# A hybrid encoder layer on one core: the merge of three branches in a written order, with eight gate tiles ahead of it

## The chip, the core and the metric

The kernel runs on one core of a Trainium2 chip. The core has five engines that work side by side: TensorE (PE, matrix products into the PSUM banks), VectorE (DVE), ScalarE (ACT), GpSimd (POOL) and SyncE (SP), which here issues all DMAs, in order, to sixteen DMA engines. Each engine works through its own queue in order and waits on semaphores for the others. The metric is the time of one execution in microseconds (us) of the device; the kernel before takes 2960.99 us, the median of three runs (2956.82 to 2964.68).

## The reference

One layer of a bidirectional encoder over 1280 tokens (a sequence of 1024 and one of 256), D_MODEL = 1024, in float32. Three mixers read the same normalised input, each is gated, and their sum goes through an output projection and a gated feed-forward network:

```python
h = rms_norm(x, p['norm_mix_g'][l])
proj = h @ p['w_in'][l]                       # split among the mixers and the gates
o_a = blocked_attention(q, k, v_a, MLA_QK ** -0.5).reshape(B, T, H * MLA_V) @ p['w_o_a'][l]
# RWKV-7, both directions, then a norm per head:
y7 = y_f + y_b
mu = jnp.mean(y7, axis=-1, keepdims=True)
var = jnp.mean(jnp.square(y7 - mu), axis=-1, keepdims=True)
y7 = ((y7 - mu) * lax.rsqrt(var + LNX_EPS)).reshape(B, T, RW_DIM)
y7 = y7 * p['lnx_g'][l].astype(F32) + p['lnx_b'][l].astype(F32)
o_b = (y7 * g7).astype(x.dtype) @ p['w_o_b'][l]
o_c = jnp.einsum('bhqk,bkhd->bqhd', pr.astype(mv.dtype), mv).reshape(B, T, X_DIM) @ p['w_o_c'][l]
gates = jax.nn.sigmoid(gate_logits.astype(F32)).reshape(B, T, N_BRANCH, D_MODEL).astype(x.dtype)
merged = gates[:, :, 0] * o_a + gates[:, :, 1] * o_b + gates[:, :, 2] * o_c
x = x + merged @ p['w_out'][l]
up = rms_norm(x, p['norm_ffn_g'][l]) @ p['w_up'][l]
# ... centred convolution of width 3 on the gate half, gelu, product, w_down
```

## The kernel before

Activations lie with the features on the 128 partitions and the tokens along the free axis; the tokens are cut into three chunks, CH: chunk 0 and chunk 1 of 512 tokens and chunk 2 of 256. Each product of float32 values is done as three matmuls of a split into a high and a low part (`mm3`, lines 133 to 135); `split` makes the parts, the cast on ACT (line 126), the difference on POOL or DVE (line 129). `load_w` (line 139) loads a weight tile by DMA and splits it.

The work comes in stages: the input projections (to about 670 us), then RWKV's scan with attention and gate tiles put between its steps (to 1648 us), the merges of the three branches (to 1936 us), the output projection (to about 2053 us) and the feed-forward network. Between stages the intermediates go through DRAM: `oaT`, `ocT` and `yS` are the mixers' outputs (attention A, cross-attention C, RWKV B), `rden` the reciprocals of the softmax sums, `gT` the gate logits, `obT` the normalised RWKV output.

RWKV's PE instructions stand in an order that the program works out beforehand: the class `Order` keeps a model time, takes the ready lane of RWKV, and where none is ready it takes the next step of a filling generator, first attention and the gate tiles of chunk 1 (`fill`), then the spare gate tiles of chunk 0 (`spare`, lines 900 to 911). A gate tile is one of 24 groups of 128 output features; in one of 512 tokens there are 24 matmuls, yielded in steps of three k, each counted as 512 x 3.6 / 1024 = 1.8 us by the planner. Before, sixteen tiles of chunk 0 (16 to 23, then 8 to 15) are on the list `g0`, and `spare` stops when four of them are left. Everywhere outside RWKV the order of the instructions on each engine is made by the compiler's list scheduler from a simulated timeline.

The merges (`merges`, line 1739; called from `phase2`): for each branch and each output tile m = 0 to 7, and for each chunk, `merge` forms `w_o` times the branch's input in PSUM (`mg_ps`), and DVE multiplies it by the gate (line 1728), which is loaded from `gT` into `mg` (line 1721) and put through tanh. The inputs are loaded by `merge_in`: a chunk of `oaT` or `ocT` (line 1699, tile `mf`, two buffers), the reciprocals, broadcast to two halves of 64 partitions (line 1704, tile `mrd`), their product on DVE (line 1707), and the split into `moh` and `mol`. Branch A comes first; between its products stand the last gate tiles: four before m = 0, one for each m whose result stays in SBUF (`keep=True`), so its chunk 0 is merged with no trip through DRAM.

`rwkv_out` (from line 1642) finishes one of the ten RWKV tiles of 128 tokens: loads of the two directions (lines 1648 and 1650, `oy` with two buffers) and of v (line 1653), the norm on DVE, POOL and ACT (lines 1661 to 1672), four PE transposes (`yt`, line 1676), scaling on ACT (1682), the product with g7 on POOL (1685) and a store into `obT`. One is called for each m of branch A and for the first two of C. Branch B, which needs all ten, is merged last; its input loads begin inside branch C.

Of the kernel before, what the change touches and what calls it, by code (L numbers as in the profile page):

```python
# [97 lines left out]
class Kern:  # L98
# [813 lines left out]

    def gates(self, p, pp):

        self.wp = p
        self.g0 = [*range(16, 24), *range(8, 16)]
        self.h[0] = self.h[1] = tuple(p.tile([128, 8, 512], F32R, name=f"gh{x}") for x in "hl")
        w = self.load_w(p, self.io["w_g"][0], [128, 8, 128], "w4", sbufs=2)
        self.gates_h(p, 1)
        yield -10.0  # L920
        for m in range(24):
            for x in self.gate_(p, pp, "at", m, 1, "go", 3, w=w):
                yield x if isinstance(x, float) else 512 * 2.4 / 1024
            w = None
# [718 lines left out]
    def rwkv_out(self, p, pr, i):  # L1643
# [14 lines left out]
        def bc(t):  # L1658
            return t.unsqueeze(2).to_broadcast([128, 8, 64])
# [29 lines left out]
    def merge_in(self, p, br, src, fs, bufs):  # L1689

        nc, io = self.nc, self.io
        for f in fs:
            oh = p.tile([128, T], F32R, tag="moh", name="moh", bufs=bufs)
            ol = p.tile([128, T], F32R, tag="mol", name="mol", bufs=bufs)
            for ci in (1, 2, 0):
                c0, cn = CH[ci]
                cs = slice(c0, c0 + cn)
                t = p.tile([128, 512], F32, tag="mf", name="mf", bufs=2)
                nc.sync.dma_start(out=t[:, :cn], in_=src[f][:, cs])
                if br != 1:  # L1700
                    rd = p.tile([128, 512], F32, tag="mrd", name="mrd", bufs=2)
                    for e in range(2):
                        r = 2 * f + e if br == 0 else 8 + f
                        nc.sync.dma_start(
                            out=rd[64 * e : 64 * e + 64, :cn], in_=io["rden"][r : r + 1, cs].to_broadcast([64, cn])
                        )
                    nc.vector.tensor_mul(out=t[:, :cn], in0=t[:, :cn], in1=rd[:, :cn])
                self.split(t[:, :cn], oh[:, cs], ol[:, cs], "act", "dve" if ci == 1 else "pool")
            yield oh, ol

    def merge_w(self, p, br, m):
        return self.load_w(p, self.io["w_o"][br][m], [128, 4, 128], "wo", sbufs=1)

    def merge(self, p, br, m, ci, w, o, merged, parts, pp, g=None):

        nc, io = self.nc, self.io
        c0, cn = CH[ci]
        cs = slice(c0, c0 + cn)
        if g is None:
            g = p.tile([128, 512], F32, tag="mg", name="mg", bufs=5 if br == 1 else 3)  # L1720
            nc.sync.dma_start(out=g[:, :cn], in_=io["gT"][br * 8 + m][:, cs])
            nc.scalar.activation(out=g[:, :cn], in_=g[:, :cn], func=AF.Tanh, scale=0.5)
        ps = pp.tile([128, 512], F32, tag="mp", name="mg_ps")
        for k in range(4):
            self.mm3(ps[:, :cn], w[0][:, k, :], w[1][:, k, :], o[k][0][:, cs], o[k][1][:, cs], k == 0, k == 3)
# [10 lines left out]
                out=lo, in0=t, scalar=0.5, in1=hi.bitcast(F32), op0=ALU.mult, op1=ALU.subtract  # L1736
            )

    def merges(self, gp, ro, mg, pp, merged):


        io = self.io

        def gate(m, keep=False):
            return self.gate(gp, pp, "mp", m, 0, "go", 3, keep)

        def gate0():
            if self.g0:
                gate(self.g0.pop(0))

        o = list(self.merge_in(mg, 0, io["oaT"], range(4), 6))
        for m in range(8):
            if m == 0:
                for _ in range(4):
                    gate0()
            w = self.merge_w(mg, 0, m)
            for ci in (1, 2):
                self.merge(mg, 0, m, ci, w, o, merged, None, pp)
            self.rwkv_out(ro, pp, m)
            g = gate(m, True)  # L1760
            self.merge(mg, 0, m, 0, w, o, merged, None, pp, g)
            gate0()
            if m == 3:
                oc = list(self.merge_in(mg, 2, io["ocT"], range(2), 6))
        for m in range(4):
            gate0()
        oc += self.merge_in(mg, 2, io["ocT"], range(2, 4), 6)
        for m in range(8):
            if m < 2:
                self.rwkv_out(ro, pp, 8 + m)  # L1770
            if m == 4:
                yield
            w = self.merge_w(mg, 2, m)
            for ci in (1, 2):
                self.merge(mg, 2, m, ci, w, oc, merged, None, pp)
            if m < 4:
                gate0()
            self.merge(mg, 2, m, 0, w, oc, merged, None, pp)


    def out_proj(self, p, x1, h2, pp):
# [157 lines left out]
    def phase2(self, rctx):  # L1939
# [8 lines left out]
        def close():  # L1948
            pools.pop().__exit__(None, None, None)
# [5 lines left out]
        with self.pool("pat", space=PSUM, bufs=3) as pa:  # L1955
# [14 lines left out]
            gctx, gp = ctx  # L1970
            close()
            x1 = left("x1").tile([128, 8, T], F32, name="x1")
            ro, mg = left("ro"), left("mgac")
            with self.pool("pmg", space=PSUM, bufs=5) as pm:
                rest = self.merges(gp, ro, mg, pm, x1)
                next(rest)
                gctx.__exit__(None, None, None)
                rctx.__exit__(None, None, None)
                wctx, mw = right("mgw")
                bctx, mb = right("mgb")  # L1980
                w = self.merge_w(mw, 1, 0)
                o = list(self.merge_in(mb, 1, io["obT"], range(4), 4))
                for _ in rest:
                    pass
                close()
                close()
                hp = left("h2")
# [4 lines left out]
                self.wu = left("wu")  # L1992
                for m in range(8):
                    wn = self.merge_w(mw, 1, m + 1) if m < 7 else None
                    for ci in range(3):
                        self.merge(mw, 1, m, ci, w, o, x1, h2, pm)
                    w = wn
                bctx.__exit__(None, None, None)
                wctx.__exit__(None, None, None)
# [3 lines left out]
        for _ in range(3):  # L2003
            close()

# [93 lines left out]
```

## Time and profile before

| | |
|---|---|
| median of three runs | 2960.99 us (2956.82 to 2964.68) |
| profiled execution, its own time | 2968.41 us |
| its span in the profile | 2966.6 us |
| PE busy in the span | 2781.4 us, 94% |
| DVE, ACT, POOL busy | 52%, 40%, 46% |
| mean granted PE clock | 0.965 of full speed |
| DMA | 261.77 MB, mean 88 GB/s |

The profile is one execution, traced by the hardware. Times count from the span's start. A row of a timeline names an engine, the line of the program, what it writes and reads, and in brackets the time for which the engine had been idle and what ended that. A row of windows gives each engine's busy time in a stretch, the granted clock of PE (1.00 is 2.4 GHz, 0.50 is 1.2 GHz), the mean busy share of the sixteen DMA engines and the rate. The share counts the time of packets, which overlap a little, so it can go above 1.

### The profile page before, as it was taken

How to read it: one execution, taken by the hardware profiler on the slowest of the kernel's cores; microseconds unless marked ns; L12 is line 12 of the kernel's file. 1: busy time of each engine (PE TensorE's matmuls, PEld its weight loads, DVE VectorE, ACT ScalarE, POOL GpSimd, SP SyncE). 2: the span in 40 equal slices, each digit the busy share in tenths (PEclk: the TensorE clock that was granted, in tenths of full speed). 3: DMA queues.
4: the chain of work that ended last, by engine and by line, in shares of the span. 5: the costliest groups of instructions: out<-in, count | busy, mean ns of one | idle time of the engine just before them, and what ended most of it. 6: DMA issues, size and time to landing. Idle time of an engine off the chain costs nothing. (4 is left out here: it accounts for less than half of the span.)

```text
span 2966.6 us, 50241 instructions
## 1 busy us (share of the span) xinstructions
PE 2781.4 (94%) x19556; PEld 2246.2 (76%) x19556; DVE 1544.2 (52%) x2576; ACT 1173.3 (40%) x2561; POOL 1358.5 (46%) x1220
## 2 busy tenths in 40 slices
PE   7998998999999999899989688999999999999999
PEld 5787787885666665477767577888888888888888
DVE  8638848566767665655565465423422323323233
ACT  5645555545555555544443234423221211212111
POOL 5546736454444344455554467743342332423323
PEclk8999999999999998899989899999999999999999
DMA  4333324553122222343343666422111111111112
GB/s 151 99 96 97 101 69 114 154 147 90 51 68 61 59 60 78 89 122 108 106 122 102 189 201 187 144 87 64 40 43 36 42 37 36 43 36 42 37 33 86
DMA packets 250005, 261.77 MB, mean 88 GB/s; under 512 B 81028, under 2 KB 178448, under 8 KB 249768
## 3 DMA queue, kind: packets, MB, share of 16 engines
q1 hardware_dynamic: 249768, 258.57, 29.6%
q8 instruction: 154, 2.52, 0.4%
q14 instruction: 83, 0.68, 0.1%
HBM read 196.64 MB, written 61.73 MB: 87 GB/s over the span
## 5 line engine op out<-in xcount | busy, mean ns | idle before, releaser
L133 PE MATMUL up<-h2h,wuh 128*128 128x512 f32 (+1 forms) x1056 | 374.2, 354 | 0.0
L134 PE MATMUL up<-h2h,wul 128*128 128x512 f32 (+1 forms) x1056 | 374.0, 354 | 0.0
L135 PE MATMUL up<-h2l,wuh 128*128 128x512 f32 (+1 forms) x1056 | 373.5, 354 | 0.0
L129 POOL TENSOR_TENSOR w4l<-w4f,w4h 128x512 fp32r<-128x512 f32 (+1 forms) x154 | 264.0, 1723 | 216.5 <-ACT w4h L126 210.4
L129 POOL TENSOR_TENSOR wul<-wuf,wuh 128x1024 fp32r<-128x1024 f32 x52 | 125.1, 2405 | 270.7 <-ACT wuh L126 270.7
L133 PEld LDWEIGHTS up<-h2h,wuh 128*128 128x128 f32 x1056 | 199.7, 189 | 28.0
L135 PEld LDWEIGHTS up<-h2l,wuh 128*128 128x128 f32 x1056 | 199.6, 189 | 27.8
L134 PEld LDWEIGHTS up<-h2h,wul 128*128 128x128 f32 x1056 | 199.7, 189 | 27.4
L1849 DVE TENSOR_TENSOR x<-x,dn 128x512 f32<-128x512 f32 (+1 forms) x192 | 113.6, 598 | 194.3 <-PE dn L135 194.3
L133 PE MATMUL proj<-hh,w4h 128*128 128x512 f32 (+1 forms) x504 | 182.2, 363 | 9.3 <-DVE go L879 5.0
L134 PE MATMUL dn<-ah,wdl 128*128 128x256 f32 (+1 forms) x528 | 187.2, 356 | 0.0
L135 PE MATMUL dn<-al,wdh 128*128 128x256 f32 (+1 forms) x528 | 184.7, 356 | 0.0
L133 PE MATMUL dn<-ah,wdh 128*128 128x256 f32 (+1 forms) x528 | 182.1, 356 | 0.4 <-ACT wdh L126 0.4
L135 PE MATMUL proj<-hl,w4h 128*128 128x512 f32 (+1 forms) x504 | 181.4, 360 | 0.0
L134 PE MATMUL proj<-hh,w4l 128*128 128x512 f32 (+1 forms) x504 | 181.0, 360 | 0.0
L126 ACT CAST w4h<-w4f 128x512 fp32r<-128x512 f32 (+1 forms) x154 | 113.2, 751 | 149.6 <-DMA w4f<-in_w_g 41.1
L133 PE MATMUL gt<-ghh,w4h 128*128 128x512 f32 x384 | 163.7, 426 | 8.3 <-ACT w4h L126 5.2
L126 ACT CAST wuh<-wuf 128x1024 fp32r<-128x1024 f32 x52 | 54.7, 1052 | 291.7 <-PE up L135 276.1
L1869 DVE TENSOR_TENSOR fraw<-up,rbc 128x512 f32<-128x512 f32 (+1 forms) x66 | 39.8, 604 | 247.7 <-PE up L135 241.0
L129 POOL TENSOR_TENSOR wdl<-wdf,wdh 128x384 fp32r<-128x384 f32 (+1 forms) x64 | 60.3, 944 | 225.1 <-ACT wdh L126 225.1
L937 DVE TENSOR_REDUCE m<-mx 128x1 f32<-128x512 f32 (+1 forms) x184 | 107.6, 601 | 105.7 <-PE mx L936 105.1
L134 PE MATMUL gt<-ghh,w4l 128*128 128x512 f32 x384 | 155.5, 405 | 7.3 <-POOL w4l L129 7.3
(392 smaller groups left out, 7418.3 us busy)
## 6 DMA issues: line engine op xcount, KB each, us to landing
w4f<-in_w_g SPq DMA_DIRECT2D x48, 512.0 KB
wuf<-in_w_up SPq DMA_DIRECT2D x44, 512.0 KB
rk<-s_rk SPq DMA_DIRECT2D x80, 192.0 KB
w4f<-in_w_g SPq DMA_DIRECT2D x48, 256.0 KB
s_gT<-go SPq DMA_DIRECT2D x40, 256.0 KB
mg<-s_gT SPq DMA_DIRECT2D x40, 256.0 KB
wdf<-in_w_down SPq DMA_DIRECT2D x48, 192.0 KB
w4f<-in_w_rw SPq DMA_DIRECT2D x30, 256.0 KB
```

What stands on the lines that cost most here:

```text
L126: nc.scalar.copy(out=hi, in_=x)
L129: (nc.gpsimd if el == "pool" else nc.vector).tensor_sub(out=lo, in0=x, in1=hi.bitcast(F32))
L133: mm(ps, lhsT=lh, rhs=rh, start=first, stop=False)
L134: mm(ps, lhsT=ll, rhs=rh, start=False, stop=False)
L135: mm(ps, lhsT=lh, rhs=rl, start=False, stop=last)
L937: nc.vector.tensor_reduce(out=m2[:, n, z : z + 1], in_=ps[:, :kn], axis=AX.X, op=ALU.max)
L1849: nc.vector.tensor_add(out=xc, in0=xc, in1=ps[:, :cn])
L1869: nc.vector.tensor_mul(out=raw[:, o : o + cn], in0=ps, in1=self.rbc[:, c0 : c0 + cn])
```

## The change

The change touches the merges and what leads to them.

- The list `g0` gets all 24 gate tiles of chunk 0, and `spare` stops when eight are left: sixteen of them are put between RWKV's steps, where before it was twelve. The last eight (0 to 7) come first in the merges, ahead of any product. They are stored in `gT` like the others and loaded again; `keep` isn't used any more.
- All PE instructions of the merges stand in the order in which the program writes them (`manual_schedule` for PE). The other engines are still ordered by the scheduler.
- `merge_in` goes by chunks: chunk 1 of all four input tiles, then chunk 2, then chunk 0, as a generator of twelve steps. Branch A's twelve steps are spread over the eight gates, C's over A's eight m, B's over C's last six. The two reciprocal loads of a chunk become one: for branch A its source pattern is two rows of `rden`, each repeated for 64 partitions, for C one row repeated for 128. Its buffers are shared with the gates' (`mg`, five).
- `rwkv_out` yields before its transposes and at its end. For each m the merges first finish the tile before (transposes to store), then begin the next, between the chunks 2 and 0. One is begun before the branches, eight in branch A, one in branch C.
- The weights of the next m are loaded while an m is merged, across branches too. The pools are laid out anew: branch C's inputs go where the gates were, `h2` and the projection's weights to the right side.

```diff
-        while len(self.g0) > 4:
+        while len(self.g0) > 8:
...
-        self.g0 = [*range(16, 24), *range(8, 16)]
+        self.g0 = [*range(16, 24), *range(8, 16), *range(8)]
...
+    def merge_in(self, p, br, src, o, order):
+
+        nc, io = self.nc, self.io
+        for ci, f in itertools.product(order, range(4)):
+            c0, cn = CH[ci]
+            cs = slice(c0, c0 + cn)
+            t = p.tile([128, 512], F32, tag="mf", name="mf", bufs=2)
+            nc.sync.dma_start(out=t[:, :cn], in_=src[f][:, cs])
+            if br != 1:
+                rd = p.tile([128, 512], F32, tag="mg", name="mrd", bufs=5)
+                n = 2 if br == 0 else 1
+                r = n * f if br == 0 else 8 + f
+                nc.sync.dma_start(
+                    out=rd[:, :cn], in_=io["rden"][r : r + n, cs].unsqueeze(1).to_broadcast([n, 128 // n, cn])
+                )
+                nc.vector.tensor_mul(out=t[:, :cn], in0=t[:, :cn], in1=rd[:, :cn])
+            self.split(t[:, :cn], o[f][0][:, cs], o[f][1][:, cs], "act", "dve" if ci == 1 else "pool")
+            yield
...
+        def out_a():
+            for i in itertools.islice(rws, 1):
+                end.append(self.rwkv_out(ro, pp, i))
+                next(end[-1])
+
+        def out_b(n):
+            while len(end) > n:
+                next(end.pop(0))
+
+        o = self.merge_o(mg)
+        ins = self.merge_in(mg, 0, io["oaT"], o, (1, 2, 0))
+        w = self.merge_w(mg, 0, 0)
         for m in range(8):
...
+            self.gate(gp, pp, "mp", self.g0.pop(0), 0, "go", 3)
+            for _ in itertools.islice(ins, 1 + m % 2):
+                pass
+        out_a()
+        gclose()
+        cctx, mc = right("mgc")
+        oc = self.merge_o(mc)
+        for br, nx, src, o, on, order in ((0, 2, io["ocT"], o, oc, (1, 2, 0)), (2, 1, io["obT"], oc, None, (0, 1, 2))):
+            if on is None:
+                on = self.merge_o(mg)
+            ins = self.merge_in(mg, nx, src, on, order)
+            for m in range(8):
+                wn = self.merge_w(mg, br if m < 7 else nx, (m + 1) % 8)
+                for ci in (1, 2):
+                    self.merge(mg, br, m, ci, w, o, merged, None, pp)
+                out_b(0)
+                out_a()
+                if nx == 2 or m > 1:
+                    next(ins, None)
+                self.merge(mg, br, m, 0, w, o, merged, None, pp)
+                if m > 1:
+                    next(ins, None)
+                w = wn
+            for _ in ins:
+                pass
+        cctx.__exit__(None, None, None)
+        return on, w
...
+            with self.pool("pmg", space=PSUM, bufs=5) as pm, self.tc.manual_schedule(engines={mybir.EngineType.PE}):
+                o, w = self.merges(gp, gclose, right, ro, mg, pm, x1)
```

## Rows read from the trace of the kernel before

**Rows 1.** Windows: length, busy time of each engine, PE's clock, DMA share and rate

```profile
1648.00:1819.00 171.00, 138.53 (x637) 113.40 (x638) 103.39 (x145) 59.03 (x114) 104.44 (x72) 0.91 0.68 201
1700.00:1819.00 119.00, 107.77 (x513) 89.66 (x512) 79.83 (x112) 45.46 (x91) 81.09 (x56) 0.96 0.66 191
1819.00:1879.00 60.00, 55.36 (x270) 46.24 (x271) 23.27 (x32) 27.76 (x53) 48.89 (x43) 0.94 0.65 201
1879.00:1936.00 57.00, 55.80 (x289) 47.49 (x288) 32.15 (x42) 25.50 (x48) 39.54 (x32) 1.00 0.39 124
```

**Rows 2.** Waits of PE, 1640 to 1940 us: total, times, longest

```profile
PE mg_ps L133 <- ACT moh L126: 16.4, 7, 6.6
PE yt L1676 <- DVE oy L1672: 15.1, 3, 6.9
```

**Rows 3.** Timeline of PE, 1680 to 1725 us: start, duration, then what it is

```profile
1685.88 0.80 PE L133 MATMUL mg_ps<-moh,woh 128*128 128x512 f32 x1 [6.56 <-ACT moh L126]
...
1698.57 1.12 PE L1676 MATMUL yt<-ident,oy 128*128 128x128 f32 x4 [6.86 <-DVE oy L1672]
...
1699.91 0.63 PE L133 MATMUL mg_ps<-moh,woh 128*128 128x512 f32 x1
...
1720.42 1.09 PE L1676 MATMUL yt<-ident,oy 128*128 128x128 f32 x4 [6.48 <-DVE oy L1672]
```

**Rows 4.** Timeline of PE, one output tile m of branch A

```profile
1734.94 0.60 PE L1676 MATMUL yt<-ident,oy 128*128 128x128 f32 x4
1735.29 0.49 PE L133 MATMUL gt<-ghh,w4h 128*128 128x512 f32 x1
...
1740.89 0.39 PE L133 MATMUL mg_ps<-moh,woh 128*128 128x512 f32 x1
...
1746.35 0.28 PE L133 MATMUL mg_ps<-moh,woh 128*128 128x256 f32 x1
...
1747.79 0.60 PE L1676 MATMUL yt<-ident,oy 128*128 128x128 f32 x4
```

**Rows 5.** Timeline of PE, RWKV's tail: first, fifth and last of six holes

```profile
1629.29 0.74 PE L1632 MATMUL dd<-Tt,pn 32*32 32x32 f32 x64 [2.27 <-DVE pn L1626]
...
1645.64 1.15 PE L1341 MATMUL ch<-W,bkt 128*64 128x64 f32 x32 [1.47 <-ACT W L1334]
...
1648.46 0.47 PE L133 MATMUL gt<-ghh,w4h 128*128 128x512 f32 x1 [0.73 <-DVE sd L1346]
```

**Rows 6.** Timeline of SP's DMA issues, from RWKV's end

```profile
1641.13 8.39 SPq L1357 DMA_DIRECT2D s_yS<-ys  x4
1649.61 0.54 SPq L1699 DMA_DIRECT2D mf<-s_oaT  x1
1650.25 1.10 SPq L1704 DMA_DIRECT2D mrd<-s_rden  x2
```

**Rows 7.** Windows, columns as in rows 1: DMA at its fullest, and branch A

```profile
1690.00:1695.00 5.00, 1.06 (x3) 0.47 (x2) 2.23 (x4) 3.26 (x6) 3.34 (x4) 0.50 1.05 381
...
1720.00:1740.00 20.00, 19.58 (x89) 16.49 (x90) 14.29 (x20) 8.21 (x17) 15.23 (x11) 0.90 0.74 217
1740.00:1760.00 20.00, 20.00 (x100) 16.94 (x99) 10.51 (x16) 7.15 (x13) 10.79 (x8) 1.00 0.77 220
```

**Rows 8.** Groups by line, 1700 to 1819 us: count, busy us, mean ns, idle before

```profile
L1661 DVE TENSOR_TENSOR oy<-oy,oy 128x512 f32<-128x512 f32 x9 | 8.1, 901 | 12.7 <-issue 7.2 <-DMA oy<-s_yS 3.8 <-PE mg_ps L135 1.6
...
L129 POOL TENSOR_TENSOR w4l<-w4f,w4h 128x1024 fp32r<-128x1024 f32 x7 | 17.3, 2471 | 4.2 <-issue 3.1 <-ACT w4h L126 1.1
```

**Rows 9.** Timeline of DVE and SP: one RWKV tile's chain, the next one's load

```profile
1745.31 0.69 DVE L1661 TENSOR_TENSOR oy<-oy,oy 128x512 f32<-128x512 f32 x1 [3.35 <-issue]
...
1754.44 0.38 SPq L1648 DMA_DIRECT2D oy<-s_yS  x1
1754.49 1.78 DVE L1672 TENSOR_TENSOR oy<-oy,lnrs 128x512 f32<-128x512 f32 x1 [1.75 <-POOL lnrs L154]
...
1759.05 0.69 DVE L1661 TENSOR_TENSOR oy<-oy,oy 128x512 f32<-128x512 f32 x1 [2.79 <-DMA oy<-s_yS]
```

More of the change, by code (lines that the diff above doesn't have):

```diff
@@ L1686, in rwkv_out, with merge_o @@
         nc.sync.dma_start(out=io["obT"][:, :, ts].rearrange("j p t -> p j t"), in_=ob)
-    def merge_in(self, p, br, src, fs, bufs):
+        yield
+    def merge_o(self, p):
+        return [tuple(p.tile([128, T], F32R, tag=f"mo{x}", name=f"mo{x}", bufs=4) for x in "hl") for f in range(4)]
+    def merge_in(self, p, br, src, o, order):
         nc, io = self.nc, self.io
[L1692 to L1709, printed above, removed]
@@ new lines, in merge_in @@
+        for ci, f in itertools.product(order, range(4)):
[12 more added lines that the diff above has]
+            self.split(t[:, :cn], o[f][0][:, cs], o[f][1][:, cs], "act", "dve" if ci == 1 else "pool")
+            yield
@@ L1711, in merge_w, with merge @@
     def merge_w(self, p, br, m):
         return self.load_w(p, self.io["w_o"][br][m], [128, 4, 128], "wo", sbufs=1)
-    def merge(self, p, br, m, ci, w, o, merged, parts, pp, g=None):
+    def merge(self, p, br, m, ci, w, o, merged, parts, pp):
         nc, io = self.nc, self.io
@@ L1718, in merge @@
         cs = slice(c0, c0 + cn)
[L1719 to L1722, printed above, removed]
+        g = p.tile([128, 512], F32, tag="mg", name="mg", bufs=5)
+        nc.sync.dma_start(out=g[:, :cn], in_=io["gT"][br * 8 + m][:, cs])
+        nc.scalar.activation(out=g[:, :cn], in_=g[:, :cn], func=AF.Tanh, scale=0.5)
         ps = pp.tile([128, 512], F32, tag="mp", name="mg_ps")
@@ L1737, in merge @@
             )
[L1739 to L1751, printed above, removed]
-        for m in range(8):
[L1753 to L1778, printed above, removed]
@@ new lines, in merges @@
+    def merges(self, gp, gclose, right, ro, mg, pp, merged):
+        io, end, rws = self.io, [], iter(range(NT))
+        def out_a():
[8 more added lines that the diff above has]
+        w = self.merge_w(mg, 0, 0)
+        for m in range(8):
+            self.gate(gp, pp, "mp", self.g0.pop(0), 0, "go", 3)
[25 more added lines that the diff above has]
+        return on, w
@@ L1972, in phase2, with gclose @@
             x1 = left("x1").tile([128, 8, T], F32, name="x1")
[L1973 to L1976, printed above, removed]
+            mg, ro = left("mgac"), left("ro")
+            def gclose():
                 gctx.__exit__(None, None, None)
                 rctx.__exit__(None, None, None)
[L1979 to L1984, printed above, removed]
+            with self.pool("pmg", space=PSUM, bufs=5) as pm, self.tc.manual_schedule(engines={mybir.EngineType.PE}):
+                o, w = self.merges(gp, gclose, right, ro, mg, pm, x1)
                 close()
-                close()
-                hp = left("h2")
+                hctx, hp = right("h2")
                 h2 = [
@@ L1991, in phase2 @@
                 ]
-                self.wu = left("wu")
+                uctx, self.wu = right("wu")
                 for m in range(8):
-                    wn = self.merge_w(mw, 1, m + 1) if m < 7 else None
+                    wn = self.merge_w(mg, 1, m + 1) if m < 7 else None
                     for ci in range(3):
-                        self.merge(mw, 1, m, ci, w, o, x1, h2, pm)
+                        self.merge(mg, 1, m, ci, w, o, x1, h2, pm)
                     w = wn
-                bctx.__exit__(None, None, None)
-                wctx.__exit__(None, None, None)
+                close()
         with self.pool("ff", side="right") as p, self.pool("psC", space=PSUM, bufs=8) as pp:
@@ L2002, in phase2 @@
             self.ffn(p, x1, h2, pp, stats)
-        for _ in range(3):
-            close()
+        uctx.__exit__(None, None, None)
+        hctx.__exit__(None, None, None)
+        close()
 def _mt(w):
```

## The prediction, made before the change was run

> **What bounds the kernel now.** I read the page's slices first: TensorE (PE) is near full from end to end except around 1600 to 1850 us, so the change, which only touches the stretch from the end of RWKV to the start of the output projection, can only win what PE loses there. The windows of that stretch [rows 1] are to be read for PE's busy time against the length: from 1648 to 1819 us PE works 138.5 of 171 us at a granted clock of 0.91, from 1819 to 1879 us 55.4 of 60 us, from 1879 to 1936 us 55.8 of 57 us. Then the waits of PE [rows 2]: it waits for the branch inputs (moh, 16.4 us) and for the normalised RWKV rows (oy, 15.1 us). The timeline says where: 6.6 us for moh and 6.9 us for oy inside 1679 to 1699 us, 6.5 us for the second oy before 1720 us [rows 3]; after such idling the clock is 0.50 and a matmul takes 0.63 us for 0.39 [rows 3, 4]. From 1735 us on PE runs through, one output tile m in 12.85 us from transpose to transpose [rows 4]. RWKV's last steps leave six holes, of 2.27, 1.89, 1.40, 0.77, 1.47 and 0.73 us, 8.5 us in all [rows 5].
>
> **Prices.** One gate tile of 512 tokens is 24 matmuls, from 1735.29 to 1740.89 us: 5.6 us; both 512-token chunks of one merge take 5.46 us (2.73 each), the 256-token one 1.44 us, one tile's four transposes 0.35 us [rows 4]. So one m costs PE 5.46 + 1.44 + 0.35 = 7.25 us without a gate.
>
> **1. Four gate tiles move into RWKV's tail.** The tail is 1626 to 1648.5 us. The planner's own costs (1.8 us for three k steps, put in whenever its model has a hole) place three whole tiles and 9 matmuls of the fourth before RWKV's last matmul: 3 x 5.6 + 2.1 = 18.9 us. Of it 8.5 us go into the holes, 10.4 us push RWKV's end from 1647.7 to 1658 us; the last 15 matmuls (3.5 us) follow, so the merges begin at 1661.5 us. The moved tiles' weights, casts and subtractions meet an idle DMA system there. Net for PE: 22.4 us of work gone from the merges, the merges 13 us later. Ends of this term: all filled 22.4 - 8.5 = 13.9 us later at most plus about 2 us if the small chain operations queue behind the gates' evacuations; no less than 11.
>
> **2. Eight gates first.** 8 x 5.6 = 45 us, to 1706.5 us if their weights arrive. Behind them the first branch's twelve chunks must be loaded, multiplied and split. SP is held by the last RWKV store until 1649.5 us, then issues the first input loads at once [rows 6]; this moves with RWKV's end, to about 1658 us. The eight tiles m = 0 to 7 of chunk 0 now go to DRAM and back (8 x 0.26 MB each way), where before they stayed in SBUF: on PE nothing, on DMA 4.2 MB.
>
> **3. The reciprocal loads, the open price.** Twenty-four loads of branch A (two of 64 partitions per chunk) become twelve whose pattern begins with a dimension of two rows, each repeated 64 times. No row shows how such a load is dealt out to the sixteen DMA engines. Low end: like the loads of before, spread over all: 2.6 MB at the 381 GB/s of a full stretch [rows 7], 7 us in all, hidden. High end: dealt out along its leading dimension, that is on two engines. One engine moves 381 / (16 x 1.05) = 22.7 GB/s [rows 7]; 64 rows of 2 KB are 131 KB, 5.8 us; eight such and four of half the length are 58 us. Everything else that shares these two engines meanwhile: input chunks 2.6 MB, four gate weights not yet prefetched 2.1, gate stores 2.1, two RWKV tiles 1.6, output weights 0.5, together 8.9 MB at 363 GB/s, 24.5 us. So the last chunk lands 82.5 us after 1658, at 1740.5 us. I take the high end, since the pair loads of the trace lead with 64 and the new pattern leads with 2: 128 packets have to be cut along some dimension, and the nearest row speaks only for patterns led by 64 or 128. Then PE, in the written order, does the gates, m = 0's chunks 1 and 2 (to about 1726, the late weights included), and stands before m = 0's chunk 0, and everything behind it, until about 1742 us. That is 31 us after the 1710.7 us at which it could have been there; 2 us more for the clock, as in rows 3.
>
> The Trainium skill has a rule on this point (DMA: Bandwidth & Descriptors, section "Why a DMA increments its semaphore by 16 and not by 1", and its "Rules for kernel authors"): the number of engines is the largest up to 16 that divides both patterns' slowest dimension that isn't 1, so a leading dimension of 2 puts the whole load on two. No row of this trace shows such a load. By that rule the sum is the one that I took; without it, the first rival's.
>
> **4. Branch A's merges with one RWKV tile per m.** Now the period p of one m counts. PE's floor is 7.25 us. DMA: 12.85 us at a share of 0.74 to 0.77 are 9.7 us of DMA time per m [rows 4, 7]; less one gate's weights (0.52 MB, 1.4 us), less half a chunk of branch C (0.6), plus the gate tile read back (0.7): 8.4 us. DVE: 79.8 us over 119 us is 8.6 us per m, less the gate's product 0.6, plus 0.6 of C's input: 8.6. POOL: 81.1 us is 8.8 per m, less the gate's subtraction (17.3 us in 9.3 m, 1.9), plus 0.6: 7.5 [rows 1, 8]. The rows' own chain: a tile's oy is loaded in 4.6 us, worked on for 11.0 us and read [rows 9]; with two buffers that allows 16.2 / 2 = 8.1 us. Nothing shows how near to the busiest of these a period can come; between 8.6 and the 13 us of today I take 9.5, a tenth over the busiest. From 1742 + 2 us: chunk 0 of m = 0 2.7 us, seven m 66.5 us: 1813 us.
>
> **5. Branches C and B.** Their inputs are loaded a branch ahead, their weights one m ahead. 60 us becomes the 24 groups' 55.3 plus two transposes and one start, 56.5 us; the last branch keeps its 57 us [rows 1]. 1813 + 56.5 + 57 = 1926.5 us, against 1935.8 before: 9.3 us less. What hides the loads is PE's 56 us per branch against 2 x 5.2 MB of gates and inputs plus 2 MB of weights, 34 us at 363 GB/s; if that cover failed, the price would be some 0.6 us per m, as the few weight waits of today.
>
> **6. At nothing.** The yields in the RWKV ends issue no instruction. The fewer reciprocal loads spare SP 24 issues of 0.55 us [rows 6]; SP is not the bound, but each input load that waits for one of the two mf buffers holds the gate weights queued behind it, which is in point 3. The h2 and weight pools change sides and neither the output projection nor the FFN does anything else. The written order adds waits on PE's own queue: behind a transpose that waits for oy stand chunk 0 of the same m and all that follows, and DVE, ACT and POOL drain with it.
>
> **Sum.** 2968.4 us is the profiled run, its span 2966.6; it lies 7.4 us over the median of 2961.0. 2968.4 - 9.3 - 7.4: 2952 us, on the edge of what a measurement of this kernel can tell from no change, 0.3%, 8.9 us. Its own range, with p from 8.5 to 10.5 and the landing some us off, is 2940 to 2964.
>
> **Rivals.**
> *The reciprocal loads are spread over all engines.* Then the stall of 31 us and the clock's 2 go; 8 us come back, since the loads done during the stall are then part of the periods: 2927. For it: all loads seen today reach rates that need all engines [rows 7]. Against: the pattern. Chance 0.2.
> *DVE and POOL exclude each other.* DVE's add of two SBUF tiles takes 0.69 us alone and 0.90 us in the mean of this stretch [rows 8, 9]. If none of DVE's five such operations per m (3.4 us) could run beside POOL's 7.3, p would be 10.7 us: 7 x 1.2 more, 2960, no difference. Against: half of them run at 0.69. Chance 0.2. The Trainium skill says so in SBUF — State Buffer, "Who interferes with whom": a DVE instruction with two SBUF inputs and a POOL instruction that reads SBUF block one another for their whole length; the stretched mean agrees.
> *Slower: the RWKV ends set the pace.* In a written order PE may not go round a late oy. The first two transposes stood 21.9 us apart, with DMA at its fullest [rows 3]; with two oy buffers p is half the time for which a tile holds one. At 26 us (16.2 today) p is 13 and the time 2952 + 24.5 = 2976. It decides from p = 12.1 (2970). For it: DMA, DVE and POOL are all within two us of PE's need, and each lengthens the chain. Against: from 1735 us on no transpose waited. Chance 0.15.
>
> **Chances.** Forecast 0.45, rivals 0.2, 0.2, 0.15. Half of the forecast lies over 0.3% faster, with the first rival 0.45 in all; within 0.3% are the second rival and most of the rest, 0.33; slower 0.22. Range 2924 to 2974: from the first rival to just short of the slowest.
>
> **What would show it.** Right: PE's tail holds gates and ends near 1658; gates until 1706 to 1726; then one long wait of PE for moh around 1726 to 1742, while DMA's mean share is far under 0.5 though loads are in flight; seven m of 9 to 10 us; 113 us from there to the projection. Wrong: a high DMA share under the gates and no wait after them (first rival); waits for oy at every m (third); a projection that begins after 1936.

## The result and the profile after

The changed kernel takes 2985.22 us, the median of four runs (2981.62 to 2996.69); against the kernel before that is a ratio of 1.0092, with a 95% interval of 1.0064 to 1.012: about 0.9% slower, where 2952 us, a gain of 0.3%, was forecast. (The ratio is taken over all runs and isn't the quotient of the two medians.) Its profiled run took 2982.88 us, with a span of 2981.1.

The places of a stage are compared in what follows from a mark that every one of these kernels has: the gate matmul that waited 1.82 or 1.83 us for a low half of its weights (1607.03 us before, 1602.24 after), to the first matmul of the output projection (1935.77 and 1950.22). I call that length **the stage**: 328.8 us before, 348.0 after, 19.2 longer. What lies ahead of the mark has the same work in both and differs by some us from profile to profile, so the stage tells more than the time does; but it is read from one profile of each kernel, and a difference of a few us in it isn't shown by that alone.

The windows of after; columns as in rows 1:

```profile
1621.00:1654.00 33.00, 32.70 (x504) 26.21 (x502) 7.73 (x14) 8.27 (x14) 11.87 (x6) 1.00 0.33 103
1659.00:1741.00 82.00, 51.21 (x176) 38.59 (x176) 27.21 (x37) 13.62 (x20) 29.74 (x19) 0.77 0.49 155
...
1741.00:1829.00 88.00, 67.08 (x323) 55.51 (x322) 61.01 (x94) 39.90 (x89) 61.69 (x47) 0.92 0.87 267
1829.00:1894.00 65.00, 58.20 (x295) 48.76 (x294) 27.21 (x38) 28.03 (x54) 56.66 (x47) 0.97 0.61 185
1894.00:1950.00 56.00, 55.71 (x290) 47.63 (x289) 29.98 (x42) 25.32 (x49) 33.85 (x29) 1.00 0.37 112
```

They are RWKV's tail (PE full: the six holes of [rows 5] are gone), the eight gates, and the branches A, C and B. PE loses 30.8 us in the gates, at a DMA share of only 0.49; 20.9 us in branch A; 6.8 us in C; nothing in B. The waits of PE from 1640 to 1980 us (engine, tile and line, releaser: us in total, times, longest) name two causes:

```profile
PE yt L1677 <- DVE oy L1672: 24.1, 8, 4.0
PE gt L133 <- ACT w4h L126: 23.5, 4, 13.4
PE gt L134 <- POOL w4l L129: 7.2, 5, 2.0
PE mg_ps L133 <- ACT moh L126: 2.7, 1, 2.7
```

Before, the first places were held by moh and oy [rows 2]; moh is nearly gone, the gates' own weights (w4h, w4l) stand in its place, and oy has grown from 15.1 to 24.1 us. The timelines of SP, DVE and PE of after show how the weights come late:

```profile
1654.70 1.09 SPq L1357 DMA_DIRECT2D s_yS<-ys  x2
...
1658.16 0.61 SPq L1707 DMA_DIRECT2D mrd<-s_rden  x1
...
1659.33 8.99 SPq L1707 DMA_DIRECT2D mrd<-s_rden  x3
1668.42 5.05 SPq L139 DMA_DIRECT2D w4f<-in_w_g  x1
...
1666.01 0.69 DVE L1710 TENSOR_TENSOR mf<-mf,mrd 128x512 f32<-128x512 f32 x1 [9.78 <-issue]
1671.85 0.69 DVE L1710 TENSOR_TENSOR mf<-mf,mrd 128x512 f32<-128x512 f32 x1 [4.55 <-DMA mrd<-s_rden]
...
1685.12 0.80 PE L133 MATMUL gt<-ghh,w4h 128*128 128x512 f32 x1 [13.45 <-ACT w4h L126]
```

The first row is RWKV's last store. Two reciprocal loads land 5.84 us apart, if the products on DVE begin when they land (for the second the profile says so; for the first it names no wait). While the first of these loads are in flight, the mean busy share of the sixteen DMA engines is 0.13, about two sixteenths, at 50 GB/s:

```profile
1664.00:1672.00 8.00, 7.67 (x34) 6.01 (x32) 1.44 (x3) 0.62 (x1) 0.39 (x1) 1.00 0.13 50
```

SP needs 8.99 us for three issues of them and 5.05 us for the one weight load behind, where the input loads of before took about 0.55 us each [rows 6]; and PE stands 13.45 us before the gate that needs such weights.

Branch A and the start of C, from the timelines of PE, SP and DVE of after (yt are the transposes of one RWKV tile, one tile per output tile m; the last two rows are C's):

```profile
1745.18 0.60 PE L1677 MATMUL yt<-ident,oy 128*128 128x128 f32 x4
1751.17 0.50 PE L133 MATMUL mg_ps<-moh,woh 128*128 128x512 f32 x1 [2.73 <-ACT moh L126]
1758.50 0.60 PE L1677 MATMUL yt<-ident,oy 128*128 128x128 f32 x4
...
1804.86 0.66 PE L1677 MATMUL yt<-ident,oy 128*128 128x128 f32 x4 [3.27 <-DVE oy L1672]
1805.55 0.33 SPq L1648 DMA_DIRECT2D oy<-s_yS  x1
1811.77 0.68 DVE L1661 TENSOR_TENSOR oy<-oy,oy 128x512 f32<-128x512 f32 x1
1815.26 0.66 PE L1677 MATMUL yt<-ident,oy 128*128 128x128 f32 x4 [2.85 <-DVE oy L1672]
1824.75 0.68 DVE L1672 TENSOR_TENSOR oy<-oy,lnrs 128x512 f32<-128x512 f32 x1
1825.49 0.66 PE L1677 MATMUL yt<-ident,oy 128*128 128x128 f32 x4 [2.68 <-DVE oy L1672]
1835.91 0.66 PE L1677 MATMUL yt<-ident,oy 128*128 128x128 f32 x4 [2.79 <-DVE oy L1672]
1847.58 0.91 PE L1677 MATMUL yt<-ident,oy 128*128 128x128 f32 x4 [4.01 <-DVE oy L1672]
```

The eight m of A have their transposes from 1745.18 to 1825.49 us: seven periods of 11.47 us in the mean; 1835.91 and 1847.58 are C's first two m. One oy buffer is freed by the transposes at 1804.86, its next load is issued at 1805.55, begun on at 1811.77 and transposed at 1825.49 to 1826.15: held 20.6 us. With two buffers that is a tile every 10.3 us, and the periods around it are 10.40, 10.23 and 10.42 us. This tile is the quickest: by their issues and transposes, the six tiles of A that reuse a buffer hold it for 20.6 to 23.2 us, 21.8 in the mean, and it lies free for 1.1 us in the mean before (4.7 the first time). Half of the sum is the 11.4 us at which the tiles follow one another. The first period, 13.32 us, has another cause: its tile was ready at 1740.56, and PE waited 3.7 us for the last input chunks of m = 0 (2.7 of it in the row at 1751.17).

### The profile page after: what moved, and what is told of

Read it like the earlier page. It is cut to its first block, busy times and chain, and to the rows that moved or that the text cites. A ratio compares the mean times of both kernels' runs of the same rounds, so it can differ in the third digit from the quotient of the medians.

```text
span 2981.1 us, 50264 instructions
## 1 busy us (share of the span) xinstructions
PE 2779.8 (93%) x19556; PEld 2244.5 (75%) x19556; DVE 1535.2 (51%) x2576; ACT 1173.0 (39%) x2561; POOL 1356.7 (46%) x1220
## 5 line engine op out<-in xcount | busy, mean ns | idle before, releaser
L1081 PE MATMUL ao<-pf,va 128*65 128x512 f32 (+1 forms) x288 | 148.1, 597 | 15.2 <-ACT os L1085 15.1
```

The lines of the kernel that those rows point to most:

```text
L1081: nc.tensor.matmul(ot[0][out, :cn], lhsT=lhsT, rhs=rhs, start=start, stop=stop)
```

## The experiments

Two causes were stated: the reciprocal loads, led by a dimension of two (theory for the gates), and the two oy buffers in a written order (theory for branches A and C). Rivals were the number of loads, DVE and POOL shutting each other out, DMA's rate and the written order itself. In the table p is the mean period of m in branch A, from the transposes of the first and the last m in it that have any (m = 0 and 7, with the lag m = 1 and 7); "rest" is from A's last transposes to the projection. The stage, p and the rest are of one profile each; ratios are against runs of the kernel before made on the same chip.

| kernel | ratio and 95% interval | median us | stage | p | rest |
|---|---|---|---|---|---|
| after | 1.0092 [1.0064, 1.012] | 2985.22 | 348.0 | 11.47 | 124.7 |
| after, two loads again | 0.9975 [0.9957, 0.9994] | 2958.32 | 319.9 | 11.06 | 126.6 |
| after, one row for two heads | 0.9952 [0.9932, 0.9971] | 2950.86 | 313.8 | 11.43 | 122.9 |
| after, three oy | 1.0054 [1.0037, 1.0071] | 2977.74 | 343.7 | 9.83 | 131.0 |
| two loads and three oy | 0.9961 [0.9948, 0.9974] | 2949.28 | 309.8 | 10.02 | 124.7 |
| two loads and three oy, no order | 0.9963 [0.9948, 0.9978] | 2955.55 | 319.3 | 10.22 | 132.9 |
| two loads, four oy, lag | 0.9921 [0.9892, 0.995] | 2943.72 | 306.5 | 9.66 | 132.2 |
| two loads, four oy, lag, gates kept | 0.9914 [0.9898, 0.993] | 2943.89 | 306.1 | 8.81 | 131.4 |
| two loads, four oy, lag, sums on DVE | 0.9936 [0.9919, 0.9953] | 2942.53 | 300.6 | 10.08 | 125.1 |

**The reciprocal loads: two again.**

```diff
-                nc.sync.dma_start(
-                    out=rd[:, :cn], in_=io["rden"][r : r + n, cs].unsqueeze(1).to_broadcast([n, 128 // n, cn])
-                )
+                for e in range(2):
+                    q = r + e * (n - 1)
+                    nc.sync.dma_start(
+                        out=rd[64 * e : 64 * e + 64, :cn], in_=io["rden"][q : q + 1, cs].to_broadcast([64, cn])
+                    )
```

> The changed kernel with one edit: the reciprocals of branch A come again in two loads of 64 partitions per chunk. Theory (a load whose pattern leads with two rows is carried by two of the sixteen DMA engines, and everything behind it waits): the long waits of PE under the eight gates (31 us for w4h and w4l) fall under 6 us, the gates end near 1705 us instead of 1741, the time falls by 20 to 33 us, to 2952 to 2965. Rival (SP's waits in order, or the plain volume of loads, starve the gates): gates end after 1730 us, the time moves by less than 6 us.

The waits of PE, 1640 to 1960 us:

```profile
PE yt L1677 <- DVE oy L1672: 27.7, 8, 6.2
PE gt L133 <- ACT w4h L126: 4.1, 1, 4.1
PE gt L134 <- POOL w4l L129: 2.3, 1, 2.3
```

The stage is 28.1 us shorter, and the gates' weights are waited for 6.4 us in place of 30.7. Branch A's period stays at 11.06 and its waits for oy with it. So the load accounts for nearly the whole of the first loss, and for little or none of the second. The time, 2958.32 us, lies in the range that was expected; the waits miss the expected 6 us by 0.4.

**The same load, led by 128.** Only one row is read, for both halves of the partitions; the second head's reciprocal is left out. Number and bytes of the loads are those of after.

```diff
-                n = 2 if br == 0 else 1
-                r = n * f if br == 0 else 8 + f
+                n = 1
+                r = 2 * f if br == 0 else 8 + f
```

> The changed kernel with branch A's reciprocal load led by 128: one row of the reciprocals goes to all 128 partitions, so the second head of each pair is scaled by the first one's reciprocal, and nothing else changes: the same number of loads, of bytes and of issues. Theory (the leading dimension of two confines the load): as with two loads of 64, the waits under the gates fall under 8 us and the time by 20 to 30 us, to 2955 to 2965. Rival (one load in place of two, its size or its place in the queue): within 6 us of the changed kernel, 2979 to 2991.

```profile
PE yt L1677 <- DVE oy L1672: 20.8, 8, 3.8
PE gt L134 <- POOL w4l L129: 5.7, 4, 2.0
```

With as many loads of as many bytes as after, the stage is 34.2 us shorter. It is the leading dimension, then, and not the number or the size. That this load reads one row and not two doesn't matter for it: with two loads both rows are read, and the loss goes too.

**The same load in the kernel before.** The diff is the first one the other way round, in the code of before, nothing else.

> The kernel before with one edit: the two reciprocal loads of a chunk become one, for branch A with a pattern that leads with two rows. Theory (two engines): the twelve loads of branch A take 5.8 us each for 512 columns, 58 us in all, and its products, of which the first began at 1667 us, wait for them: 15 to 35 us slower than before, 2976 to 2996. Rival (the load is spread like the others): within 5 us of before, a little faster for 24 issues less.

Measured: 2987.14 us, a ratio of 1.008 [1.0054, 1.0106], a stage of 350.5 us, 21.7 longer than before. Two of its waits of PE:

```profile
PE mg_ps L133 <- ACT moh L126: 17.3, 6, 7.2
PE gt L133 <- ACT w4h L126: 7.9, 2, 4.4
```

By itself the one line costs as much as the whole change lost (19.2 us of stage), as expected (2976 to 2996 us). PE is idle 12.4 us longer in this stage than before and busy 9.4 us longer, at a granted clock of 0.91 in place of 0.93. The inputs are waited for hardly longer than before (17.3 us for 16.4), the gates' weights 7.9 us, a wait that before doesn't have; the rest isn't traced.

**Three oy buffers.**

```diff
-        y = p.tile([128, 8, 64], F32, tag="oy", name="oy", bufs=2)
+        y = p.tile([128, 8, 64], F32, tag="oy", name="oy", bufs=3)
```

> The changed kernel with one edit: oy has three buffers instead of two. Theory (branch A's period of 11.2 us is the time that a tile holds one of two oy buffers, 20 us, halved): the waits of the transposes for oy (24.1 us in eight) fall under 8 us, the period to 9.5 us or less, the time by 10 to 18 us, to 2967 to 2975. Rival (DMA at a share of 0.87 and DVE and POOL set the period, oy is only where it shows): waits move to other places, the period stays over 10.7 us, the time moves by less than 5 us.

Transposes of branch A, the last row C's (timeline of PE):

```profile
1762.28 0.60 PE L1677 MATMUL yt<-ident,oy 128*128 128x128 f32 x4
...
1784.32 0.60 PE L1677 MATMUL yt<-ident,oy 128*128 128x128 f32 x4
1792.17 0.66 PE L1677 MATMUL yt<-ident,oy 128*128 128x128 f32 x4
...
1837.10 0.66 PE L1677 MATMUL yt<-ident,oy 128*128 128x128 f32 x4 [2.34 <-DVE oy L1672]
```

The waits for oy fall from 24.1 to 6.2 us, three m in a row take 22.04 us, close to PE's floor of 7.25 us each, and the mean p falls from 11.47 to 9.83: in the changed kernel the two buffers held branch A up. But they weren't the only bound. Three buffers let one more tile be loaded under the gates, and more got ahead while PE waited for inputs in the first period (17.85 us); once that start is used up, the four periods from 1792.17 to 1837.10 take 11.2 us in the mean. The pace of the tiles themselves is better seen on POOL, in the subtraction of L1667, one per tile. From the fifth tile to the tenth it comes every 11.1 us in after, every 10.5 us here, and every 10.3 to 10.8 us in the later versions with three or four buffers and the written order: the buffers gave a start and little more pace. Of the 11.5 us that A's seven periods are shorter, 4.3 are left at the end of the stage. The rest of it is 6.3 us longer, with a new wait of PE, for the low halves of the output weights on POOL (wol, 9.1 us). The time, 2977.74 us, lies between the two expectations.

**Both mends.** The diffs of the first and the third experiment together.

> Both edits. If the two losses add up (31 us and 13 us): 2940 to 2950, faster than the kernel before. If the loads that the stall under the gates had covered now press on branch A, DMA becomes its bound: the period is 11 us or more, and the time is within 5 us of the run with two loads alone.

Measured: the stage is 38.2 us shorter than after's and the time, 2949.28 us, under that of before, as expected if the losses add up. The two give 5.8 us more together than the sum of each alone (28.1 and 4.3); why isn't settled by these runs.

**Part 1 alone.** The kernel before, with all its spare gates of chunk 0 put between RWKV's steps:

```diff
-        while len(self.g0) > 4:
+        while len(self.g0) > 0:
```

> The kernel before with one part of the change alone: the spare list is put between RWKV's steps to its end, so four gate tiles leave the merges' start for RWKV's tail. Theory (8.5 us of holes are filled, the four gates had covered the first loads of branch A): the holes go, the first products wait longer for moh; 0 to 9 us faster, 2953 to 2963. Rival (PE was the bound of the merges' start): 10 us or more faster.

Measured: 2970.81 us, 1.0021 [1.0004, 1.0039], a stage of 334.2, 5.4 longer, where both expectations were a gain. Its longest waits of PE:

```profile
PE mg_ps L133 <- ACT moh L126: 22.8, 9, 5.0
PE mg_ps L133 <- ACT woh L126: 9.9, 2, 9.4
```

Filling the six holes wins nothing where the gates taken for it had covered the first loads of the merges: PE is through with RWKV and the gates, and then has nothing until the weights (9.4 us in one wait) and the inputs are in. In the changed kernel the eight gates are that cover.

**No written order.** Both mends, without the manual schedule in the merges:

```diff
-            with self.pool("pmg", space=PSUM, bufs=5) as pm, self.tc.manual_schedule(engines={mybir.EngineType.PE}):
+            with self.pool("pmg", space=PSUM, bufs=5) as pm:
```

> The kernel with two loads and three oy buffers, without the written order for PE in the merges: the scheduler orders it. If the written order costs time by holding PE behind late transposes (14.7 us of waits for oy): 5 to 12 us faster, 2937 to 2945. If the written order is what helps: 3 us or more slower, over 2952. If neither matters: within 3 us of 2949.

Measured: a ratio of 0.9963, the written order's being 0.9961, with intervals that cover each other; PE waits 31.2 us for oy in place of 14.7, and the stage of this one profile is 9.5 us longer. By the ratio the two can't be told apart. The medians, 2949.28 with the order and 2955.55 without, and the profile lean to the order; that it is worth something is suggested, not shown.

**More lag.** Four oy buffers, and each tile's transposes one m later:

```diff
-                out_b(0)
+                out_b(0 if br == 2 and m > 1 else 1)
```

> The kernel with two loads and three oy buffers, with each RWKV tile finished one m later and a fourth oy buffer. Theory (the transposes wait for the chain's length, not for throughput): the waits for oy go from 14.7 us to under 4, the time falls by 5 to 12 us, to 2937 to 2944. Rival (DMA is the bound of branch A, at shares of 0.89 to 1.10): the waits move to the weights, the inputs or the gates, and the time stays within 4 us of 2949.

```profile
PE mg_ps L134 <- POOL wol L129: 13.4, 8, 3.9
PE yt L1677 <- DVE oy L1672: 3.7, 2, 3.1
```

```profile
1660.00:1780.00 120.00, 101.68 (x469) 82.16 (x468) 90.77 (x131) 50.80 (x100) 85.04 (x61) 0.95 0.95 282
```

These are its waits of PE and its window of gates and branch A. The wait for oy is nearly gone and the time is in the range that was expected for that. The ratio is 0.9921, and its interval lies below that of the two loads alone; it touches that of both mends (0.9948 to 0.9974), so that the lag and the fourth buffer gain anything over these is likely and not shown. The largest wait is now wol, on POOL, in A and the start of C. The DMA share of 0.95 over 120 us looked like the next bound.

**Is it DMA?** Chunk 0's gate tiles stay in SBUF, 4.2 MB less to move:

```diff
-            self.gate(gp, pp, "mp", self.g0.pop(0), 0, "go", 3)
+            kept.append(self.gate(ro, pp, "mp", self.g0.pop(0), 0, "kg", 8, True))
...
-                self.merge(mg, br, m, 0, w, o, merged, None, pp)
+                self.merge(mg, br, m, 0, w, o, merged, None, pp, kept[m] if br == 0 else None)
```

> The kernel of e7_lag (three parts changed from the kernel after: two loads of 64 partitions for branch A's reciprocals, four oy buffers, the last two tiles of A put behind the start of branch C) with one thing more: the eight gate tiles of chunk 0 stay in SBUF after they are computed, and the merges read them there instead of storing them to DRAM and loading them again for each tile. That takes away some 4.2 MB of traffic of the gate and merge stages. Theory (in e7_lag the DMA engines set the pace of the gates and of branch A: its rows show a share of 0.91 to 1.09 there, at about 275 GB/s): the time falls by 8 to 15 us against e7_lag, to 2929 to 2936, and the DMA share of branch A falls. Rival (the chain of one tile or the engines set the pace, and the DMA share is high only because the work behind it is elastic): within 4 us of e7_lag's 2944.

```profile
1660.00:1780.00 120.00, 107.15 (x490) 87.25 (x489) 81.18 (x121) 46.49 (x88) 80.02 (x57) 0.94 0.81 236
```

The share fell to 0.81, as it should, and p to 8.81; the time didn't move (2943.89 against 2943.72), nor did the stage (306.1 and 306.5). The theory has fallen: what the six periods of A won (5.1 us) had been lost ahead of them, the first transposes coming 5.5 us later after the mark (121.8 against 116.3), and the wait for wol stayed (11.9 us). Whether fewer bytes shortened the periods or the later start did isn't told apart. The next two tried the same from another side: RWKV tiles begun at every second m of A only, alone and with the gates kept.

```diff
-                out_b(0 if br == 2 and m > 1 else 1)
-                out_a()
+                out_b(0 if br == 2 and m > 4 else 1)
+                if br == 2 or m % 2 == 0:
+                    out_a()
```

> The kernel of e7_lag, but in branch A an RWKV tile is begun only at every second m, so that five of them are loaded and computed in A instead of nine, and the rest follow in the first m's of branch C, where the DMA share was 0.6. No byte and no instruction is added or left out; some 4 MB of loads, and the VectorE and GpSimd work on them, move from A to C. Theory (DMA engines set the pace of A): A becomes 12 to 18 us shorter, C at most 5 us longer, and the time falls by 8 to 15 us against e7_lag, to 2929 to 2936. Rival (A is paced by something else, or C takes what A gives): within 4 us of 2944, with C longer by what A is shorter.

> Both edits at once: gate tiles of chunk 0 kept in SBUF (as e9_keep) and RWKV tiles begun at every second m of branch A (as e10_spread). Theory (DMA engines set the pace): the first of the two brings most of what there is until TensorE's own floor for branch A (7.25 us for one m) is reached, so the sum is less than both: 2920 to 2932. Rival (something else sets the pace): within 4 us of e7_lag's 2944.

Measured: 2946.62 us (0.9929 [0.9913, 0.9946], stage 306.0) and 2954.34 us (0.9948 [0.9927, 0.997], stage 312.3): no gain. The first fits its rival, the second is slower than both of its expectations. Three ways of taking load from DMA in branch A, and none shortened the stage by as much as a microsecond.

**Is it POOL?** Branch C's sums on VectorE, the version with the lag:

```diff
         if br == 2:
-            nc.gpsimd.tensor_add(out=mc, in0=mc, in1=t)
+            nc.vector.tensor_add(out=mc, in0=mc, in1=t)
```

> The kernel of e7_lag with branch C's sums (L1734, 24 additions of 1.14 us, 27 us of GpSimd) on VectorE instead, which is busy 5 to 12 us of each 20 us in C while GpSimd is busy 15 to 20. In e7_lag TensorE's largest wait of the stage is for GpSimd's lower halves of the output weights (13.4 us, 8 times). Theory (after the loads, the buffers and the lag are mended, GpSimd sets the pace of the end of A and of C): that wait falls below 5 us, the stage from the last gate tiles to the projection becomes 6 to 13 us shorter than e7_lag's 306.5, and the time falls to 2931 to 2938. Rival (GpSimd's queue is late only because its inputs are, so that another wait takes over at once): the stage stays within 4 us of 306.5 and the time within 4 us of 2944.

```profile
PE mg_ps L134 <- POOL wol L129: 13.9, 9, 3.7
```

```profile
1768.93 0.61 ACT L126 CAST woh<-wof 128x512 fp32r<-128x512 f32 x1
1769.11 1.27 POOL L129 TENSOR_TENSOR mol<-mf,moh 128x512 fp32r<-128x512 f32 x1 [1.28 <-ACT moh L126]
1770.48 2.01 POOL L154 TENSOR_TENSOR lnrs<-lnms,mhalf 128x8 f32<-128x8 f32 x1
1772.46 1.26 POOL L129 TENSOR_TENSOR wol<-wof,woh 128x512 fp32r<-128x512 f32 x1
1773.78 0.80 PE L134 MATMUL mg_ps<-moh,wol 128*128 128x512 f32 x1 [3.67 <-POOL wol L129]
...
1786.92 0.50 PE L134 MATMUL mg_ps<-moh,wol 128*128 128x512 f32 x1 [3.51 <-POOL wol L129]
...
1793.48 0.68 DVE L1734 TENSOR_TENSOR x<-x,mg 128x512 f32<-128x512 f32 x1
```

These are its largest wait of PE, the timelines of ACT, POOL and PE at one such wait, a later one, and the first of the moved sums on DVE. Neither expectation is met in full. The wait stayed at 13.9 us. But 11.1 us of it, the wait at 1786.92 included, come before the first moved sum at 1793.48: nothing was taken from POOL ahead of them, so this run doesn't test whether POOL's load makes them. What it shows of one wait is this: woh is ready at 1769.54, and POOL, which takes its work in order and itself waited 1.28 us for moh, puts a split of the next branch's input and an RWKV step before wol. There at least the order has a part. Behind the first moved sum the rest of the stage is 7.1 us shorter (125.1 against 132.2) and the stage 5.9, which is what less load on POOL would do. The time doesn't show it: 0.9936 and 0.9921, intervals that overlap. Of the versions that beat both kernels, the four with the lag that lie between 2942.5 and 2946.6 us can't be told apart.

## Why the prediction was wrong, by its steps

The forecast put the start of the projection at 1926.5 us; in after's profile, whose mark is 4.8 us earlier, that is 1921.7. It came at 1950.2, 28.5 us later. The steps share it as follows.

- **1, RWKV's tail: right.** PE is full there (32.70 of 33 us), and RWKV's end, forecast at 1658 - 4.8 = 1653.2, shows in its last store, issued from 1654.70 on. That the cover of the first loads goes with them was not in the prediction; with the eight gates behind no such wait is seen here, alone it costs (part 1 alone, +5.4 us of stage).
- **2 and 3, the gates and the load: right in mechanism and size, wrong in the place.** Landing 5.8 us apart was forecast and 5.84 measured; 31 us of standing, and 30.8 were found in the gates, at a DMA share that was 0.13 while the first loads were in flight. By the rule of the Trainium skill (DMA: Bandwidth & Descriptors, "Why a DMA increments its semaphore by 16 and not by 1") this is a load on two engines; the two experiments on the leading dimension agree with it, 28.1 and 34.2 us. But PE stood before the gates' own weights, queued behind the loads on SP, not behind the gates: the products of m = 0's chunks 1 and 2, 4.2 us, came after the standing and not before it. Branch A's chunk 0 began at 1745.5, against 1744 - 4.8 = 1739.2: 6.3 us, 4.2 of it from the place.
- **4, the period of branch A: the step that failed.** Taken 9.5, measured 11.47: 7 x 1.97 = 13.8 us. Of these 3.8 are the first period, where PE waited for the last input chunks, and 10.0 the other six, 11.2 us in the mean. The sentence at fault is the one on the chain, 16.2 / 2 = 8.1: I read the 16.2 us, a tile's load, chain and transposes with no wait between, from a stretch where DMA was at 0.74 to 0.77 [rows 7, 9]. (With its wait for PE the tile of rows 9, loaded from 1740.50 on and transposed until 1761.21, held its buffer 20.7 us even there, but no transpose waited for it.) At 0.87 the quickest tile held its buffer 20.6 us: 6.2 until work on it began in place of 4.6, 13.7 at work in place of 11.0, and 0.7 for the transposes themselves. DVE and POOL are hardly busier than before, 0.69 and 0.70 of the window against 0.67 and 0.68 [rows 1]; how much of the 4.4 us is DMA's and how much DVE's and POOL's queues isn't told apart. Half of 20.6, 10.3, is a bound that 9.5 lies under, and with the mean of 21.8 and the free time it is 11.4. The other half of the step, a tenth over the busiest engine, was too short as well: with three buffers p was 9.83 and 10.02, but with tiles made ready under the gates in it, and no version with the written order brought the fifth to the tenth tile through POOL faster than one in 10.3 us. What sets that pace stays open.
- **5, branch C: mis-sized, 65.7 for 56.5.** Here the same chain was overlooked: two RWKV tiles are transposed in C's first two m, and the periods that end with these transposes took 10.42 and 11.67 us where PE needs 7.25 each: 7.6 of the 9.2 us. **B: right**, 55.8 for 57.

6.3 + 13.8 + 9.2 less 1.2 in B are 28.1 of the 28.5 us. The forecast of 2952 with 28.5 on it is 2980.5. What is left to the median of 2985.2 has nothing to do with the stage: the profiled run lay 7.4 us over the median before and 2.3 under it after, 9.7 together, less the 4.8 us by which the mark came earlier.

**The rivals.** *Loads spread over all engines*: made so by hand, the kernel takes 2958 or 2951 us, not 2927; p is 11.06 or 11.43 there and not 9.5, which is 10.9 or 13.5 us of it, and C's first two m are as slow as in after. *DVE and POOL shut each other out*, p at least 10.7: neither shown nor refuted. With the gates kept p is 8.81, but in those six periods, 1729.18 to 1782.03, POOL subtracted for only five tiles (L1667), more having been ready before, and from the fifth tile to the tenth that step comes every 10.3 us:

```profile
1749.70 1.42 POOL L1667 TENSOR_TENSOR oy<-oy,mu 128x512 f32<-128x512 f32 x1
...
1801.01 1.03 POOL L1667 TENSOR_TENSOR oy<-oy,mu 128x512 f32<-128x512 f32 x1
```

The rival's 10.7 lies within the 10.3 to 10.8 us of the versions with more buffers, and no run took the exclusion away. *The RWKV ends set the pace*: its mechanism is what happened, at 20.6 to 23.2 us of holding and not 26, and waits for oy at nearly every m were the sign it named. Its price was put on top of a sum in which A's other terms and C were right; it needed p = 12.1 to make the change slower, and with C's 9.2 and the place of the gates' wait 11.47 did.

So the change loses by one pattern: with that load mended, the same kernel is on the other side of before (0.9975, and 0.9952 where one row serves two heads). That the buffers keep it from more is seen in the stage (4.3 and 10.1 us for the third one) and not clearly in the time, where the intervals touch; that the written order costs or gives anything is not shown.

## What to carry to other kernels

Where a change merges two loads into one, look at what dimension now leads the pattern: a small one slows that load and everything queued behind it on SP, and the loss shows up at another tile (here the gate weights). Where an order is written out, compute for each rotating buffer the time it is held under the new load, not the old, and divide by the count; take it as a lower bound of the period also in the branch after. When buffers are added, look at the late tiles and not at the mean: the first ones may only have been made ready ahead. A high DMA share is no bound until less traffic has been seen to shorten the stage. And to test whether an engine's load makes a wait, take the load away ahead of that wait.

## What the runs showed of the hardware

A load of 256 KB led by a dimension of two landed 5.84 us after the one before it, by the products behind them; the rate is 45 GB/s, about two sixteenths of the 381 GB/s of a full stretch [rows 7], and the mean share of the sixteen engines was 0.13 meanwhile. The DMA share reads above 1 over whole stretches: the version with the lag has, from 1760 us,

```profile
1760.00:1780.00 20.00, 12.44 (x52) 9.83 (x52) 16.12 (x23) 10.71 (x23) 17.34 (x13) 0.85 1.09 318
```

and 1.05 went with 381 GB/s before [rows 7]: the rate that goes with a full share depends on what is moved. A subtraction on POOL that meets an addition of two SBUF tiles on DVE is longer, in the same version:

```profile
1721.28 0.68 DVE L1661 TENSOR_TENSOR oy<-oy,oy 128x512 f32<-128x512 f32 x1
1721.44 1.42 POOL L1667 TENSOR_TENSOR oy<-oy,mu 128x512 f32<-128x512 f32 x1 [0.71 <-DVE mu L1666]
...
1792.29 1.03 POOL L1667 TENSOR_TENSOR oy<-oy,mu 128x512 f32<-128x512 f32 x1
```

1.42 us beside the addition, which began first and kept its 0.68 us, against 1.03 where no DVE instruction runs. The rule that the prediction weighed (the Trainium skill, SBUF — State Buffer, "Who interferes with whom") fits such pairs; whether as a sum over an m it sets a bound here isn't shown.
